# A hybrid attention layer on one core: the end rebuilt, and small work on the vector and scalar engines moved behind other work

## The chip, the cores and the metric

The kernel runs on one core of a Trainium2 chip. Its engines run side by side, each through a fixed list of instructions in order: TensorE (PE, matrix products), VectorE (DVE, elementwise work), ScalarE (ACT, copies, functions, squares with sums), GpSimd (POOL) and SyncE (SP, which here only issues transfers; POOL and ACT issue some too). Semaphores tie the lists together. The metric is the device time of one execution in microseconds (us), as the median of three runs.

## The reference

One decoder layer over 512 tokens of width 2048, in float32. Half of the heads are latent attention (MLA), half are forgetting attention (FoX); both are gated, their outputs go through one projection, and a normalised result is added to x:

```python
h = _rms_norm(x, g_pre)
q_lat, kv_lat, k_rope_raw, gate_mla, fq, fk, fv, f_logit, gate_fox = jnp.split(h @ w_in, split_points, axis=-1)
o_mla = _mla_branch(q_lat, kv_lat, k_rope_raw, ...) * jax.nn.silu(gate_mla)
o_fox = _fox_branch(fq, fk, fv, f_logit, b_forget) * jax.nn.silu(gate_fox)
o = jnp.concatenate([o_mla, o_fox], axis=-1) @ w_out
return x + _rms_norm(o, g_post)
```

In the MLA half, queries, keys and values come from normalised latents (`w_uq`, `w_ukv`), and part of each query and key is rotated by position. In the FoX half, running sums of log-sigmoids of `f_logit` are added to the scores.

## The kernel before

**Arithmetic.** A float32 product is made of three fast products of high and low halves (`mm3`, L153 to L156): high by high, high by low, low by high. Each weight chunk is loaded into `raw`, its high half `whi` is cast by ACT (L295), and its low half `wlo` is the difference that DVE takes (L298). PE meets a chunk first with `whi`, a little later with `wlo`.

**Products.** Four projections go through a scheme with seven block products in place of eight, named p1, p2, p4, q6, g7, g5 and g3: FoX values and gates (`v`, `g`), latents and MLA gate (`l`, `m`), MLA values (`u`) and the output (`o`). Their operands are sums of blocks of x, of latents or of weights, so there are many 128x512 additions and subtractions on DVE between the products.

**Order.** The program is written once, in straight order; a scheduler then makes one static list for each engine from its own estimates of durations. Two things steer it: `in_order` (L136) keeps an instruction where the program has it, and `todo` (L608) is a queue of small steps of which `pump` takes one or two after each group of matmuls, so that a step's place in the program is set by its place in the queue. `wait(n)` hands out pauses.

**The places that matter here**, in the order of time:

- Opening (about 50 to 80 us). The `fq` products run; `todo` gets sums of x (`x_sums`, tiles `rmg`, `smg`) and the log-sigmoid steps `fs` (tile `rft`) from L1329. At the end of the chain PE transposes `rft` into bank `rf` (L878), and DVE copies it out and scans it. Behind `fq` come the products `va` of values from chunks `rawv` and `ga` of gates.
- Latents (about 570 to 580 us). When product g5 of `l` ends, four additions `lc <- ls, lc` (L1400, called from L1461) are issued at once, ahead of the low half of the next chunk; PE then works on MLA-gate products `mg` and on queries `mq` of the first MLA pair.
- First MLA pair (590 to 620 us). `mla_q` (L1727) makes queries, casts and rotates them; then p1 of `u` fills the banks `uA`, which ACT copies to `up`; keys `mk` follow; then q6 (banks `uC`, from operand `suq`), p2 (`uA` again), p4 (`uB`) and g7 (`uC`), with scores `sm` of the heads between.
- Fourth MLA pair (about 702 us). Attention outputs are divided into halves (`boa`) by steps put at the front of `todo` (L1783).
- End (from about 840 us). The last product is p2 of `o` for the second half of the columns, banks `oa10` (token tile 0) and `oa11` (token tile 1). `held=3` keeps its last three weight chunks ready so that tile 0 is ended before tile 1 on them. `finish` (L1857) takes the sum of squares of a row (`sso`), the inverse root y (tile `fin`), multiplies by the gain `gp`, adds x (`xr`) and stores to `out`. The two later token tiles (2 and 3) are finished earlier; tile 0 and then tile 1 come last. For tile 1 the four quarters of the columns are: quarter 0 on PE (x and the scaled values are added in bank `mix`, ACT copies it out), quarters 1, 3 and 2 on DVE (`SCALAR_TENSOR_TENSOR`, below STT: values times y plus x).

Of the kernel before, what the change touches and what calls it, by code (L numbers as in the profile page):

```python
# [19 lines left out]
P = 128  # L20
D = 2048
# [44 lines left out]
def tile_hybrid_layer(  # L66
# [50 lines left out]
    def split(src, name, scale=None, first=0):  # L117

        both = parts_of[name] = slot(name, F32R)
        hi, lo = both[:, 0, :], both[:, 1, :]  # L120
        split_into(hi[:, first:], lo[:, first:], src[:, first:], scale)
        return hi, lo

    def whole_block(wholes, i, src, scale=None):

        to = wholes[:, i // 4, i % 4 * P : (i % 4 + 1) * P]
        if scale is None:
            act.copy(to, src[:, :P])
        else:
            act.mul(to, src[:, :P], scale)  # L130
# [22 lines left out]
    def mm3(o, ah, al, bh, bl, first, last, **kw):  # L153
        pe.matmul(o, ah, bh, start=first, stop=False, **kw)  # L154
# [132 lines left out]
    def divide(i):  # L287
# [4 lines left out]
        hi = wp.tile([P, 1024], F32R, tag="whi", name=f"whi{i}")  # L292
        lo = wp.tile([P, 1024], F32R, tag="wlo", name=f"wlo{i}")
# [157 lines left out]
    for n in ("q0", "p1", "k0", "q6", "p2", "p4", "g7", "q1", "g5", "k1", "g3", "q2", "k2", "q3", "k3"):  # L451
# [184 lines left out]
    def proj_T(rng, outs, kh, kl, rate=1, ahead_load=4):  # L636
# [3 lines left out]
        for i in rng:  # L640
            hi, lo = chunk(i, ahead_load)
            for j in range(chunks[i][3]):
                for o, rows, pick in outs:
                    mm3(o[:rows, :], pick(hi, j), pick(lo, j), kh[k], kl[k], k == 0, k == n_k - 1)
# [190 lines left out]
    def forget_sums(r):  # L835
# [39 lines left out]
        def rows():  # L875
            pt = att_bank("rf")
            for t in range(NT):
                pe.transpose(pt[:n, t * P : (t + 1) * P], r[:, t * n : (t + 1) * n], ident)  # L878
# [156 lines left out]
    def away_steps(of, j, pair, plain=(), keep=None):  # L1035
# [14 lines left out]
        def make(i, n, x, y, names=None):  # L1050
# [3 lines left out]
            dve.tensor_tensor(out=blocks[n], in0=blocks[x], in1=blocks[y], op=ALU.subtract)  # L1054
# [274 lines left out]
    todo.extend([*x_sums(0), *fs[3:], *x_sums(1)])  # L1329
# [94 lines left out]
    def products(gs, names, between, out=lambda g, c, half: None):  # L1424
# [3 lines left out]
        for name in names:  # L1428
            for g in gs:
# [332 lines left out]
    for p in range(4):  # L1762
# [4 lines left out]
        q, qw, wholes = mla_q(p)  # L1767
        if p == 0:
            A = [proj_bank("uA0"), bank("pv", "uA1", 1)]
            up_product("p1", latent_x(0, 0), A, True)  # L1770
            p1 = slot("up1")
            for t in range(2):
                act.copy(p1[:, t, :], A[t])
            p1 = halves(p1)
        elif p == 1:
# [6 lines left out]
        else:  # L1782
            todo.extendleft(divisions("a12", "o"))  # L1783
# [11 lines left out]
        ]  # L1795
        enqueue_scores(heads)
# [250 lines left out]
```

## Time and profile before

| | us |
|---|---|
| Median of three runs (lowest to highest) | 887.06 (886.84 to 887.31) |
| The profiled execution | 887.44 |
| Its span in the profile | 885.6 |
| DVE busy | 643.5 |
| ACT busy | 507.0 |
| POOL busy | 124.3 |
| Granted TensorE clock, mean | 0.999 |

The profile is of one execution. The span runs from the first to the last recorded event; the execution's own time is 1.8 us longer. Records of consecutive matmuls overlap (a matmul of 512 columns is recorded with 0.39 us, but the next one starts 0.227 us after it), so a wait of PE is read from the distance between two starts. In a view of the timeline a row has the start, the duration, the engine, the line, the operation, the tiles (result `<-` operands) and the shapes; `xN` stands for N instructions in one row, and in brackets stands idle time of the engine with what ended it.

### The profile page before, as it was taken

The numbers are of one execution on the slowest core, as the hardware profiler recorded it, in microseconds if no ns is written. First come the engines' busy times: TensorE is split into PE (matmuls) and PEld (weight loads), VectorE is DVE, ScalarE is ACT, GpSimd is POOL, SyncE is SP. The second block draws the span as 40 slices with busy tenths as digits, with TensorE's granted clock in tenths as the row PEclk, the third lists the DMA queues.
The fourth block names the chain that finished last, engine by engine and source line by source line (L and its number), as shares of the span: only waits on it lengthen the run. The fifth ranks groups of instructions, "written<-read, shape, count | busy, mean of one in ns | idle before, by whom it ended". The sixth has DMA issues, their size and how long they took to land.

```text
span 885.6 us, 13146 instructions
## 1 busy us (share of the span) xinstructions
PE 874.2 (99%) x4724; PEld 753.5 (85%) x4724; DVE 643.5 (73%) x1120; ACT 507.0 (57%) x933; POOL 124.3 (14%) x131
## 2 busy tenths in 40 slices
PE   9999999999999999999999999999999999999997
PEld 9988888888888888889999999887888788888885
DVE  4789567778475645547667778899778777998786
ACT  7855444444276553545564455649585986655483
POOL 0024014441010101000024433100000000000030
PEclk9999999999999999999999999999999999999999
DMA  9599879999587898984789999887969537699787
GB/s 291 162 303 276 284 200 195 224 231 238 103 199 216 226 219 208 244 216 131 267 293 239 230 215 258 179 230 164 215 160 246 138 130 253 198 333 331 258 220 236
DMA packets 129158, 198.37 MB, mean 224 GB/s; under 512 B 16370, under 2 KB 62092, under 8 KB 128068
## 3 DMA queue, kind: packets, MB, share of 16 engines
q1 hardware_dynamic: 101956, 136.09, 48.8%
q0 software_dynamic: 26256, 61.02, 35.3%
q8 instruction: 37, 0.61, 0.3%
q10 hardware_dynamic: 880, 0.42, 0.2%
q14 instruction: 29, 0.24, 0.1%
HBM read 182.60 MB, written 44.25 MB: 256 GB/s over the span
## 4 chain that ended last, share of the span: by engine, by line
PE 86%; DVE 6%; ACT 4%; DMA 3%; issue 1%; SPq 0%; DVEq 0%; ACTq 0%
PE gg L1122 3%; PE fk L154 3%; PE fk L156 3%; PE fk L155 3%; PE fq L154 3%; PE fq L156 3%; PE fq L155 3%; PE in L679 2%; PE sm L725 2%; PE lg L1122 2%; DMA rawl<-in_w_in_dram 2%; PE mg L156 2%; PE gg L1123 2%; PE mg L155 2%; PE mg L154 2%; PE ga L1122 2%
## 5 line engine op out<-in xcount | busy, mean ns | idle before, releaser
L298 DVE TENSOR_TENSOR wlo<-raw,whi 128x1024 fp32r<-128x1024 f32 (+3 forms) x159 | 186.7, 1175 | 91.8 <-ACT whi L295 86.6
L295 ACT CAST whi<-raw 128x1024 fp32r<-128x1024 f32 (+3 forms) x158 | 160.0, 1017 | 158.4 <-PE fk L155 43.3
L154 PE MATMUL fk<-h,whi 128*128 128x512 f32 x128 | 51.3, 401 | 0.0
L154 PE MATMUL fq<-h,whi 128*128 128x512 f32 x128 | 50.4, 394 | 0.0
L156 PE MATMUL fk<-h,wlo 128*128 128x512 f32 x128 | 50.1, 392 | 0.0
L156 PE MATMUL fq<-h,wlo 128*128 128x512 f32 x128 | 50.1, 391 | 0.0
L155 PE MATMUL fq<-h,whi 128*128 128x512 f32 x128 | 50.1, 391 | 0.0
L155 PE MATMUL fk<-h,whi 128*128 128x512 f32 x128 | 49.9, 390 | 0.0
L295 ACT CAST whi<-rawv 128x1024 fp32r<-128x1024 f32 x24 | 25.2, 1052 | 37.2 <-PE gg L1122 18.7
L295 ACT CAST whi<-rawl 128x1024 fp32r<-128x1024 f32 x25 | 26.2, 1050 | 35.2 <-PE mg L155 10.4
L298 DVE TENSOR_TENSOR wlo<-rawl,whi 128x1024 fp32r<-128x1024 f32 x25 | 30.5, 1222 | 19.8 <-ACT whi L295 19.8
L295 ACT CAST whi<-rawg 128x1024 fp32r<-128x1024 f32 x24 | 25.3, 1052 | 30.5 <-PE vg L156 15.3
L298 DVE TENSOR_TENSOR wlo<-rawv,whi 128x1024 fp32r<-128x1024 f32 x24 | 29.2, 1219 | 16.5 <-ACT whi L295 16.2
L298 DVE TENSOR_TENSOR wlo<-rawg,whi 128x1024 fp32r<-128x1024 f32 x24 | 29.2, 1222 | 13.1 <-ACT whi L295 13.1
L745 ACT ACTIVATE pf<-pf,stf 128x128 f32<-128x128 f32 (+3 forms) x32 | 17.9, 559 | 22.5 <-DVE stf L736 22.5
L1854 POOL DMA_DIRECT2D c<-in_x_dram x8 | 7.0, 1012 | 168.1 <-ACT c L1853 168.1
L679 PE MATMUL in<-whi,h 128*128 128x328 f32 x128 | 29.8, 326 | 0.0
L247 POOL DMA_DIRECT2D rawl<-in_w_in_dram x20 | 23.9, 1193 | 41.4 <-DVE wlo L298 31.3
L154 PE MATMUL mq<-ln,whi 128*128 128x512 f32 x72 | 29.0, 403 | 0.5 <-ACT whi L295 0.5
L156 PEld LDWEIGHTS fk<-h,wlo 128*128 128x128 f32 x128 | 24.0, 188 | 5.3
L156 PEld LDWEIGHTS fq<-h,wlo 128*128 128x128 f32 x128 | 24.0, 188 | 5.1
L155 PE MATMUL mq<-ln,whi 128*128 128x512 f32 x72 | 28.2, 392 | 0.0
(605 smaller groups left out, 2792.7 us busy)
## 6 DMA issues: line engine op xcount, KB each, us to landing
raw<-in_w_in_dram SPq DMA_DIRECT2D x62, 512.0 KB
raw<-in_w_out_dram SPq DMA_DIRECT2D x32, 512.0 KB
rawl<-in_w_in_dram POOLq DMA_DIRECT2D x20, 512.0 KB, 10.9
rawv<-in_w_in_dram POOLq DMA_DIRECT2D x16, 512.0 KB, 9.0
rawg<-in_w_in_dram POOLq DMA_DIRECT2D x16, 512.0 KB, 10.7
raw<-in_w_in_dram POOLq DMA_DIRECT2D x12, 512.0 KB, 9.8
bmg<-awaymg SPq DMA_DIRECT2D x20, 256.0 KB
rawl<-in_w_in_dram SPq DMA_DIRECT2D x10, 512.0 KB
```

The source lines that it names most:

```text
L154: pe.matmul(o, ah, bh, start=first, stop=False, **kw)
L155: pe.matmul(o, ah, bl, start=False, stop=False, **kw)
L156: pe.matmul(o, al, bh, start=False, stop=last, **kw)
L247: pool.dma_start(to, second, accum_op=ALU.add)
L295: act.copy(hi[:, :m], raw[:, :m])
L298: dve.tensor_tensor(out=lo[:, :m], in0=raw[:, :m], in1=hi[:, :m].bitcast(F32), op=ALU.subtract)
L679: pe.matmul(banks[t][:, :n], a[k][:, tss[t]], b[:, j, :], start=k == 0 and m == 0, stop=k == NK - 1 and m == 2,)
L725: m = pe.matmul(s[:, :nn], a[:, qs], c[:, :nn], start=(i == 0), stop=(i == len(pairs) - 1))
L745: act.activation(p, p, AF.Exp, bias=st[:, 0:1], scale=unit, accum_out=st[:, 1:2])
L1122: pe.matmul(o[t][f], hi[:, j, c], both, start=first and kk == 0, stop=False, skip_group_check=True)
L1123: pe.matmul(o[t][f][:, :HALF], lo[:, j, c], both[:, 0, :], start=False, stop=last and kk == 7, skip_group_check=True,)
L1854: pool.dma_start(to, x[piece(t, c)], accum_op=ALU.add)
```

## The change

Six places of the program are edited.

1. Opening: the steps of `fs` go ahead of all sums of x in `todo`, behind ten empty steps; the transposes into `rf` and the subtractions of the first two sums are kept in program order.
2. Latents: the four additions behind g5 of `l` become steps of `todo`; those of the other projections stay.
3. First MLA pair: p2 and p4 of `u` come ahead of q6 (also in the list by which chunks are loaded); p1's copies are kept in order and put between the casts and the rotation of the queries; the first matmul of each query chain is kept in order; two pauses stand ahead of the scores.
4. Fourth MLA pair: the divisions of `boa` are spread, one in every second place of `todo` from the sixth on.
5. Last chunk: its halves get tiles of their own in the freed pool `op`, so that they needn't wait for a `whi` and a `wlo` to come free; `held` is 4; one bank (`oh1`) for a gained value goes, and the value stays in its own tile.
6. `finish`: the root is taken by ACT straight from the sum (scale and bias in the instruction), while DVE computes v; y is then 2w/(w² + v) in place of 1/w with one Newton step. Tile 0: quarters 3 and 2 on DVE, 0 and 1 as an ACT multiplication and a POOL addition each. Tile 1: three pieces of 256 columns on PE and ACT, five on DVE; the gain of quarter 2 stands ahead of its two pieces.

```diff
-    todo.extend([*x_sums(0), *fs[3:], *x_sums(1)])
+    todo.extend([*[lambda: None] * 10, *fs[3:], *x_sums(0), *x_sums(1)])
...
-                pe.transpose(pt[:n, t * P : (t + 1) * P], r[:, t * n : (t + 1) * n], ident)
+                in_order(pe.transpose(pt[:n, t * P : (t + 1) * P], r[:, t * n : (t + 1) * n], ident))
...
-                    put(g, 1, 0, a, ALU.add)
-                    put(g, 1, 1, a, ALU.add)
+                    adds = [lambda g=g, c=c, a=a: put(g, 1, c, a, ALU.add) for c in range(2)]
+                    if g == "l":
+                        todo.extend(adds)
+                    else:
+                        for add in adds:
+                            add()
...
-    for n in ("q0", "p1", "k0", "q6", "p2", "p4", "g7", "q1", "g5", "k1", "g3", "q2", "k2", "q3", "k3"):
+    for n in ("q0", "p1", "k0", "p2", "p4", "q6", "g7", "q1", "g5", "k1", "g3", "q2", "k2", "q3", "k3"):
...
-            up_product("p1", latent_x(0, 0), A, True)
             p1 = slot("up1")
-            for t in range(2):
-                act.copy(p1[:, t, :], A[t])
+            def first_up():
+                up_product("p1", latent_x(0, 0), A, True)
+                for t in range(2):
+                    in_order(act.copy(p1[:, t, :], A[t]))
+            q, qw, wholes = mla_q(p, first_up)
...
-            todo.extendleft(divisions("a12", "o"))
+            for i, s in enumerate(divisions("a12", "o")):
+                todo.insert(6 + 2 * i, s)
...
+        if i < len(chunks) - 1:
+            hi = wp.tile([P, 1024], F32R, tag="whi", name=f"whi{i}")
+            lo = wp.tile([P, 1024], F32R, tag="wlo", name=f"wlo{i}")
+        else:
+            hi, lo = (more[0].tile([P, 1024], F32R, tag="raw", name=f"w{n}{i}", bufs=3) for n in ("hi", "lo"))
...
-    product("p2", 1, operand("a12", "o"), A2, False, True, held=3, side=[end2])
+    product("p2", 1, operand("a12", "o"), A2, False, True, held=4, side=[end2])
```

The core of the new `finish`:

```python
        act.activation(w, sso[:, t, 3:4], AF.Sqrt, bias=u, scale=1.0 / D)
        dve.tensor_scalar(out=v, in0=sso[:, t, 3:4], scalar1=1.0 / D, scalar2=u, op0=ALU.mult, op1=ALU.add)
        in_order(dve.tensor_scalar(out=q, in0=w, scalar1=w, scalar2=v, op0=ALU.mult, op1=ALU.add))
        in_order(dve.reciprocal(q, q))
        in_order(dve.tensor_scalar(out=y, in0=q, scalar1=w, scalar2=2.0, op0=ALU.mult, op1=ALU.mult))
...
        if t < LAST:
            done(3, whole)
            gained()
            done(2, whole)
            for c in (0, 1):
                act.mul(homes[c], og[t][c], y)
                pool.tensor_tensor(out=homes[c], in0=homes[c], in1=xr[t][c], op=ALU.add)
                nc.sync.dma_start(out[piece(t, c)], homes[c])
            return
        mixes = [(proj_bank("mix0"), 1, left), (proj_bank("mix1"), 0, left), (att_bank("mix2"), 0, right)]
...
        for mix, c, at in mixes:
            act.copy(homes[c][:, at], mix[:, :HALF])
            act.dma_start(out[piece(t, c)][:, at], homes[c][:, at])
        done(1, right)
        done(3, left)
        done(3, right)
        gained()
        done(2, left)
        done(2, right)
```

Three places of the static lists, before and after. DVE in the opening, before: `rft` is the log-sigmoid chain, `rmg` and `smg` are sums of x, `wlo` low halves of weights, `rf` the copy of the transposed result.

```order
L864 RECIPROCAL rft_647<-rft_647 128x32
L298 TENSOR_TENSOR wlo13_784<-rawv0_678,whi13_783 128x1024
L848 TENSOR_TENSOR rft_647<-rft_647 128x32
L1054 TENSOR_TENSOR rmg51_819<-xr01_618,xr11_619 128x512
L848 TENSOR_TENSOR rft_647<-rft_647 128x32
L845 TENSOR_SCALAR rft_647<-rft_647 128x32
L1054 TENSOR_TENSOR rmg51_819<-xr01_618,rmg51_819 128x512
L848 TENSOR_TENSOR rft_647<-rft_647 128x32
L144 TENSOR_TENSOR smg51_821<-rmg51_819,smg51_821 128x512
L848 TENSOR_TENSOR rft_647<-rft_647 128x32
L1054 TENSOR_TENSOR rmg31_833<-xr11_619,rmg51_819 128x512
L851 SCALAR_TENSOR_TENSOR rft_647<-rft_647 128x4x8
```

After, from the same point of the chain (the reciprocal):

```order
L868 RECIPROCAL rft_647<-rft_647 128x32
L852 TENSOR_TENSOR rft_647<-rft_647 128x32 x2
L849 TENSOR_SCALAR rft_647<-rft_647 128x32
L852 TENSOR_TENSOR rft_647<-rft_647 128x32 x2
L855 SCALAR_TENSOR_TENSOR rft_647<-rft_647 128x4x8
L302 TENSOR_TENSOR wlo13_774<-rawv0_678,whi13_773 128x1024
L849 TENSOR_SCALAR rft_647<-rft_647 128x4x8
L883 COPY rf_167<-rf_802 72x512
L302 TENSOR_TENSOR wlo14_813<-rawv1_680,whi14_812 128x1024
L889 SCALAR_TENSOR_TENSOR fz_808<-rf_167,fz_808 8x512
L1058 TENSOR_TENSOR rmg50_823<-xr00_528,xr10_529 128x512
L143 TENSOR_TENSOR smg50_825<-rmg50_823,smg50_825 128x512
```

The sums of x stood between the steps of the chain; now the chain runs through, and the first of them stand behind the copy of `rf`, a chunk's low half and the scan `fz`.

ACT in the first MLA pair, before. `up` is p1 of `u` copied out of the banks `uA`, `suq` and `sug` are operands of q6 and g7, `rq` the rotated queries, `mw` and `mk` parts of the keys, `mc` a gate function behind the table load.

```order
L143 CAST rq0_5963<-raq0_5955 64x512 x2
L143 CAST suq60_5985<-ruq60_5941 128x512
L143 CAST sug30_5999<-rug30_5988 128x512
L1773 COPY up1_6004<-uA0_5968 128x512
L1773 COPY up1_6004<-uA1_5969 128x512
L143 CAST sug70_6024<-rug70_6002 128x512
L128 COPY mw0_5952<-mk00_6007 128x128
L128 COPY mw0_5952<-mk01_6008 128x128
L143 CAST mk00_6055<-mk00_6007 128x512
L143 CAST mk01_6058<-mk01_6008 128x512
L295 CAST whi160_6068<-raw160_5873 128x1024
L295 CAST whi161_6151<-raw161_5915 128x1024
```

After, from the copies of `up` on, to the copy `u11` that empties the first `uA` bank after p2:

```order
L299 CAST whi160_6066<-raw160_5876 128x1024
L127 COPY mw0_5955<-mk01_6008 128x128
L299 CAST whi161_6125<-raw161_5918 128x1024
L142 CAST rq0_6002<-raq0_5994 64x512 x2
L142 CAST sug70_6024<-rug70_5990 128x512
L811 ACT_TABLE_LOAD
L811 ACTIVATE mc0_4139<-ghm0_6027 128x512
L811 ACTIVATE mc0_4139<-ghm1_6037 128x512
L142 CAST mk00_6055<-mk00_6007 128x512
L142 CAST mk01_6058<-mk01_6008 128x512
L748 ACTIVATE stm00_6085<-stm00_6085,qcol_3813 128x1
L1820 COPY u11_6118<-uA0_5828 128x512
```

The cast of `suq` stood behind two casts of `rq`, right ahead of the copies `up`; now it stands ahead of the copies `up`, six places ahead of the first row shown, and the copy `u11` stands behind `whi161`, two casts of `rq`, one of `sug`, the table load, two gate functions and the casts of `mk`.

DVE in the last stretch, before: `fin0` and `fin1` are the small columns for the root of tiles 0 and 1, `xr` is x, `oa10` and `oa11` are the last product.

```order
L1913 SCALAR_TENSOR_TENSOR og20_8661<-oa10_7285,fin0_8709,xr02_8652 128x512
L1913 SCALAR_TENSOR_TENSOR c121_8287<-c121_8287,fin0_8709,xr02_8652 128x512
L1913 SCALAR_TENSOR_TENSOR c120_8022<-c120_8022,fin0_8709,xr00_8649 128x512
L1864 TENSOR_SCALAR fin1_8748<-sso_7280,fin1_8748 128x1
L1866 TENSOR_SCALAR fin1_8748<-fin1_8748 128x1
L1872 TENSOR_TENSOR oa11_7286<-oa11_7286,gp1_7282 128x128
L1875 RECIPROCAL fin1_8748<-fin1_8748 128x1
L1877 TENSOR_SCALAR fin1_8748<-fin1_8748 128x1
L1878 TENSOR_SCALAR fin1_8748<-fin1_8748 128x1
L1901 SCALAR_TENSOR_TENSOR c120_8022<-oh1_8553,fin1_8748,xr10_8655 128x256 x2
L1872 TENSOR_TENSOR oa11_7286<-oa11_7286,gp1_7282 128x384
L1913 SCALAR_TENSOR_TENSOR c121_8287<-oh3_8682,fin1_8748,xr12_8658 128x512
```

After, from the first STT of tile 0:

```order
L1896 SCALAR_TENSOR_TENSOR c121_8287<-c121_8287,fin0_8700,xr02_8649 128x512
L1892 TENSOR_TENSOR oa10_7285<-oa10_7285,gp1_7282 128x512
L1896 SCALAR_TENSOR_TENSOR og20_8658<-oa10_7285,fin0_8700,xr02_8649 128x512
L1884 TENSOR_SCALAR fin1_8745<-sso_7280,fin1_8745 128x1
L1885 TENSOR_SCALAR fin1_8745<-fin1_8745 128x1
L1886 RECIPROCAL fin1_8745<-fin1_8745 128x1
L1887 TENSOR_SCALAR fin1_8745<-fin1_8745 128x1
L1896 SCALAR_TENSOR_TENSOR c120_8022<-c120_8022,fin1_8745,xr10_8652 128x256
L1896 SCALAR_TENSOR_TENSOR c121_8287<-oh3_8667,fin1_8745,xr12_8655 128x256 x2
L1892 TENSOR_TENSOR oa11_7286<-oa11_7286,gp1_7282 128x512
L1896 SCALAR_TENSOR_TENSOR og20_8658<-oa11_7286,fin1_8745,xr12_8655 128x256 x2
```

The third STT of tile 0 is gone from DVE, as are one small column step and the gain of 128 columns between the root's steps; tile 1 has one STT of 256 columns on `c120` where there were two.

More of the change, by code (lines that the diff above doesn't have):

```diff
@@ L151, in split_into, with mm3 @@
             in_order(a, b)
-    def mm3(o, ah, al, bh, bl, first, last, **kw):
-        pe.matmul(o, ah, bh, start=first, stop=False, **kw)
+    def mm3(o, ah, al, bh, bl, first, last, pin=False, **kw):
+        i = pe.matmul(o, ah, bh, start=first, stop=False, **kw)
+        if pin:
+            in_order(i)
         pe.matmul(o, ah, bl, start=False, stop=False, **kw)
@@ L1868, in finish @@
+        homes = [og_tile(t, c) for c in range(4)]
         og[t][last] = o
-        sides = (slice(0, P), slice(P, S)) if t == LAST else (slice(0, S),)
-        def gain_side(at):
-            return dve.tensor_tensor(out=o[:, at], in0=o[:, at], in1=gp[last][:, at], op=ALU.mult)
-        in_order(gain_side(sides[0]))
-        dve.reciprocal(y, w)
-        dve.tensor_scalar(out=w, in0=y, scalar1=y, scalar2=h, op0=ALU.mult, op1=ALU.mult)
-        dve.tensor_scalar(out=y, in0=w, scalar1=1.5, scalar2=y, op0=ALU.add, op1=ALU.mult)
@@ L1879, in finish @@
-        if t == LAST:
-            mix = att_bank("mix")
-            scaler = op.tile([P, P], F32, tag="sc", name="scaler", bufs=1)
-            pe.matmul(mix, ident, xr[t][0], start=True, stop=False)
-            busy = att_bank("busy")
-            for n in (S, HALF):
-                pe.matmul(busy[:, :n], ident, xr[t][1][:, :n], start=True, stop=True)
-            act.mul(scaler, ident, y)
-            pe.matmul(mix, scaler, og[t][0], start=False, stop=True)
-        order = enumerate((0, 1, 3, 2))
@@ new lines, in finish @@
+        mixes = [(proj_bank("mix0"), 1, left), (proj_bank("mix1"), 0, left), (att_bank("mix2"), 0, right)]
+        scaler = op.tile([P, P], F32, tag="sc", name="scaler", bufs=1)
+        for mix, c, at in mixes:
+            pe.matmul(mix[:, :HALF], ident, xr[t][c][:, at], start=True, stop=False)
+        busy = att_bank("busy")
+        pe.matmul(busy[:, :HALF], ident, xr[t][1][:, left], start=True, stop=True)
+        act.mul(scaler, ident, y)
+        for mix, c, at in mixes:
+            pe.matmul(mix[:, :HALF], scaler, og[t][c][:, at], start=False, stop=True)
@@ L1994, in end @@
         sub(v, G, halves(v), ALU.add)
-        done_with(0, 2 * g + 1, halves(v), {1: home})
+        done_with(0, 2 * g + 1, halves(v), {1: home} if home is not None else {})
     C = [proj_bank(f"oc{t}") for t in range(2)]
@@ L2003, in tile_hybrid_layer @@
     product("g3", 0, operand("g3", "o"), G, False, True)
-    end(0, v, G, bank("pv", "oh1", 1))
+    end(0, v, G, None)
     product("g3", 1, operand("g3", "o"), G2, False, True)
```

92 lines of the change are left out of this document (42 added, 50 removed).

## The prediction

> **What bounds the kernel.** I read the page first, then the waits of PE, then the timeline around each wait.
>
> ```profile
> span 885.6 us, 13146 instructions
> PE 874.2 (99%) x4724; PEld 753.5 (85%) x4724; DVE 643.5 (73%) x1120; ACT 507.0 (57%) x933; POOL 124.3 (14%) x131
> ...
> PE uC L154 <- ACT suq L143: 1.6, 1, 1.6
> ...
> PE mix L1888 <- ACT scaler L1887: 1.0, 1, 1.0
> PE mk L154 <- ACT mw L128: 0.7, 1, 0.7
> PE mq L154 <- ACT whi L295: 0.5, 1, 0.5
> PE rf L878 <- DVE rcol L1547: 0.3, 1, 0.3
> PE pvm L154 <- DVE mc L776: 0.2, 1, 0.2
> ```
>
> PE works through 99% of the span, and the change takes no product away. So there are only two stocks to win from: these waits, some 4 us together, and the tail behind the last product. Each of the edits aims at one row. The sum is made against the profiled execution, 887.44 us (the span of 885.6 and 1.84 around it); the median is 887.06, so 0.38 comes off at the end.
>
> **Opening.**
>
> ```profile
> 54.52 0.34 DVE L864 RECIPROCAL rft<-rft 128x32 f32<-128x32 f32 x1
> 58.86 0.69 DVE L1054 TENSOR_TENSOR rmg<-xr 128x512 f32<-128x512 f32 x1
> 59.46 0.17 DVE L845 TENSOR_SCALAR rft<-rft 128x32 f32<-128x32 f32 x1
> ...
> 59.08 0.39 PE L156 MATMUL fq<-h,wlo 128*128 128x512 f32 x1
> 59.78 0.38 PE L878 MATMUL rf<-ident,rft 128*72 128x128 f32 x2 [0.31 <-DVE rcol L1547]
> ...
> 69.30 1.22 DVE L298 TENSOR_TENSOR wlo<-rawv,whi 128x1024 fp32r<-128x1024 f32 x1
> 73.41 0.39 PE L155 MATMUL va<-wlo,h 128*128 128x512 f32 x1
> ```
>
> From 59.08 to 59.78 are 0.70 us where a 512-column matmul takes 0.23 to the next start, so PE loses 0.47. Between the reciprocal and the last step of `rft` (54.52 to 59.46) DVE makes five sums of x like that of 58.86, 0.6 to 0.7 each. Without them the chain ends over 3 us earlier, so the 0.47 goes. The eight sums come back behind the scan, where DVE makes the halves of the `va` chunks. By my reckoning the half of 69.30 then ends near 72.9 in place of 70.5, and PE asks for it near 73.4 (73.41, less 0.47, plus two matmuls by which the new order of PE asks later). That cover of half a microsecond is thin, and the next half, for `ga`, has no more. Value 0.45; range 0 (each tenth that DVE is later there comes back as a wait) to 0.55.
>
> **Latents.**
>
> ```profile
> 570.15 2.48 DVE L1400 TENSOR_TENSOR lc<-ls,lc 128x512 f32<-128x512 f32 x4
> 572.55 1.21 DVE L298 TENSOR_TENSOR wlo<-raw,whi 128x1024 fp32r<-128x1024 f32 x1
> ...
> 571.44 0.28 PE L155 MATMUL mg<-bmg,whi 128*128 128x256 f32 x1
> 572.22 0.50 PE L154 MATMUL mq<-ln,whi 128*128 128x512 f32 x1 [0.50 <-ACT whi L295]
> ```
>
> PE breaks off `mg` at 571.44, since the low half it wants next is made only at 572.55, behind four additions that take 2.48; it goes over to `mq`, which waits too. From 571.08 to 579.90 PE issues 48 matmuls of 256 columns (0.12 each) and 9 of 512 (0.23): 7.83 of 8.82 us, so 0.99 is lost. With the additions behind the half, that half is ready near 571.3. But ACT's high half of the next chunk and the `mq` behind it stay where they are, and about half of the loss with them. Value 0.5; range 0 to 1.0.
>
> **First MLA pair.** This is the largest wait, and the least certain term.
>
> ```profile
> 599.03 0.39 PE L156 MATMUL mk<-ln,wlo 128*128 128x512 f32 x1
> 601.01 0.50 PE L154 MATMUL uC<-whi,suq 128*128 128x512 f32 x1 [1.59 <-ACT suq L143]
> ...
> 599.05 1.26 ACT L143 CAST rq<-raq 64x512 fp32r<-64x512 f32 x2 [3.94 <-DVE raq L1735]
> 603.17 1.10 ACT L143 CAST mk<-mk 128x512 fp32r<-128x512 f32 x2
> 604.12 2.04 ACT L295 CAST whi<-raw 128x1024 fp32r<-128x1024 f32 x2
> 606.18 1.28 ACT L807 ACT_TABLE_LOAD   x1
> 607.48 1.16 ACT L807 ACTIVATE mc<-ghm 128x512 f32<-128x512 f32 x2
> ...
> 599.26:609.54 10.28, 8.69 (x43) 6.96 (x43) 10.15 (x16) 10.12 (x17) 0.00 (x0) 1.00 0.46 84
> ```
>
> (The last row is a window: length, then busy time of PE, weight loads, DVE, ACT and POOL.) PE loses 1.75 at 601.01 because `suq` stands behind `rq`, and `rq` behind the rotation; with small losses up to 609 it is 2.3. Now p2 comes first and needs only ready latents; `suq` has four more microseconds. So this wait goes. What is late next is the end of the same group. By the order, the second bank of `uC` is `uA`'s old one: it waits for the copy `u11`. ACT takes `whi161` only when PE has ended p2, whose `whi158` it overwrites: p2's twelve matmuls start from 599.26 on, the last at 601.75, and with its 0.39 that is 602.15. Then follow, start to start, `whi161` 1.0, two `rq` 1.25, `sug` 0.5, the table load 1.3, two `mc` 1.1, two `mk` 0.95, a small step 0.25 and the copy itself 0.5: 6.9, so the bank is free near 609.1. PE gets there after p2, p4 and half of q6, 30 matmuls from 599.26, or 606.1, with 0.5 of scores between (and one wait of 0.5 for DVE's maximum): 607.1. The new wait is 2.0, with the 0.5 it is 2.5, against 2.3. The window says why: DVE and ACT are both busy for 98% of this stretch, so a new order of PE can hardly shorten it. Value −0.2; range −1.5 to +2.0 (the upper end if the copy is not waited for).
>
> [...] The rows show the load at 606.18 and the next function at 607.48, 1.30 apart, and no drain ahead of it (the casts of 604.12 end at 606.16). [...]
>
> **Fourth pair.**
>
> ```profile
> 702.36 0.63 ACT L143 CAST boa<-boa 128x512 fp32r<-128x512 f32 x1
> ```
>
> PE's wait for `mw` (0.7) and for `mc` (0.2) stand in the first fence: `boa` casts of 0.5 each are in ACT's way. Spread out, they leave the first place but come later, ahead of scores' work; the chunk that follows is then as late as before. Value 0.2; range −0.3 to 0.6.
>
> **The end.**
>
> ```profile
> 875.07 1.68 POOL L1911 TENSOR_TENSOR og<-og,xr 128x512 f32<-128x512 f32 x1 [12.06 <-issue]
> 875.54 1.76 DVE L1913 SCALAR_TENSOR_TENSOR c<-c,fin,xr 128x512 f32<-128x512 f32 x1
> 876.40 0.19 ACT L1839 ACTIVATION_READ_ACCUMULATOR osq<-oa 128x1 f32 x1
> 877.22 0.20 DVE L1864 TENSOR_SCALAR fin<-sso,fin 128x1 f32<-128x1 f32 x1
> 877.46 0.20 ACT L1865 ACTIVATE fin<-fin 128x1 f32<-128x1 f32 x1 [0.86 <-DVE fin L1864]
> 877.72 0.15 DVE L1875 RECIPROCAL fin<-fin 128x1 f32<-128x1 f32 x1
> 877.91 0.27 DVE L1877 TENSOR_SCALAR fin<-fin 128x1 f32<-128x1 f32 x1
> 878.22 0.21 DVE L1878 TENSOR_SCALAR fin<-fin 128x1 f32<-128x1 f32 x1
> 878.47 0.88 DVE L1901 SCALAR_TENSOR_TENSOR c<-oh,fin,xr 128x256 f32<-128x256 f32 x2
> 878.93 1.12 PE L1888 MATMUL mix<-og,scaler 128*128 128x512 f32 x2 [0.96 <-ACT scaler L1887]
> ...
> 881.28 0.35 ACTq L1905 DMA_DIRECT2D out_dram<-og  x1
> ...
> 881.45:883.40 1.95, 0.00 (x0) 0.00 (x0) 0.00 (x0) 0.00 (x0) 0.00 (x0) 1.00 1.02 362
> ```
>
> The sum of squares is there at 876.59, yet the root begins at 877.22: DVE is held by an STT of tile 0 that took 1.76 beside POOL's addition. Now tile 0's sum closes 24 matmuls (5.4 us) ahead of the last, not 18; its third STT goes to ACT and POOL, and DVE is free near 874.3. So root and v both start at 876.65. The steps then take 0.26 (root), 0.31, 0.19 and 0.25, in the spacings of the rows: y's first user starts at 877.65, not 878.47. From there five STTs of 256 columns (0.4 each) and a gain of 512 (0.6) end near 880.3; on the other side scaler 0.46, three PE pieces of half the 1.12 each, copies and issues put the last issue of ACT near 880.6, against 881.28. The stores behind it flow at 362 GB/s until 883.40 (the last row), because the view of DMA issues has 768 KB in the last four, from 880.5 on; now 512 KB are in the last four, spread over 0.7 us and issued earlier, and they are through near 882.3. Value 1.1; range 0.4 (only the earlier y, with a late bank or low half) to 1.4. A fourth held chunk asks for its low half 1.4 us earlier; I find it ready with 0.1 to spare.
>
> [...] If any DVE work beside POOL were stretched as in the row of 875.54, it would be 0.4.
>
> **Sum.** 0.45 + 0.5 − 0.2 + 0.2 + 1.1 = 2.05 less; 887.44 − 2.05 − 0.38 = **885.0**.
>
> **Rivals.** (1) The copy `u11` is not waited for, or comes early: then 2.2 more, 882.8. For it: the wait that goes is the profile's largest. Against: the order of ACT. (2) Opening and latents give nothing, the waits move on to the `va`, `ga` and `mq` halves: 0.95 less gain, 886.0. For it: DVE's thin cover of half a microsecond. (3) The tail keeps its length, because tile 0's POOL additions, two in place of one, reach into tile 1's STTs (1.02 more, as in the row of 875.54): 886.0. Against: they should end by 876.5. [...] (5) Slower: DVE, at 98% between 599 and 609, becomes the bound, because the rotation (six operations) now stands ahead of the low halves `wlo159` and `wlo160` for PE's next products. Each microsecond that DVE lags is one of PE. Up to 2 us the wait at `u11` hides it; from 4 us of lag the gains elsewhere are used up. At 6 us it is 889.0.
>
> **Chances.** Forecast 50%, (1) 15%, (2) 11%, (3) 8%, (4) 4%, (5) 12%. About 0.2% (1.8 us) is what a measurement of this kernel can tell from no change; the border is 885.3, inside the forecast's own range of 884.2 to 885.9, of which I put 60% below. Faster: 30 + 15 = 45%. Same: 20 + 11 + 8 + 4 = 43%. Slower: 12%. The range leaves out (5) and half of (1): 882.9 to 887.1.
>
> **What would show it.** Right: no gap ahead of `rf`; `mg` unbroken at 571; a wait of about 2 us of `uC` on ACT's `u11`; the first STT of tile 1 1.25 us behind the start of the sum's read-out (876.40 here), not 2.07; last issue about 0.7 earlier. Wrong: PE waits at `wlo` of `va` or `ga`, at `uB` or `uC` on a low half, or a stretched STT of tile 1.

## The result: slower by 0.7%, and the profile after

| | before | after |
|---|---|---|
| Median, us (lowest to highest of nine runs each) | 887.06 (886.65 to 891.31) | 893.61 (890.74 to 895.60) |
| Ratio after to before, with its 95% interval | | 1.0066 (1.0055 to 1.0077) |
| The profiled execution, us | 887.44 | 893.61 |
| Its span, us | 885.6 | 891.8 |

The kernel became slower, by 6.5 us in the medians and 6.2 us in the two profiled spans. The page and the waits of PE after the change (line waited for, us in total, times, longest):

```profile
span 891.8 us, 13167 instructions
...
PE 876.2 (98%) x4730; PEld 755.7 (85%) x4730; DVE 642.2 (72%) x1114; ACT 507.5 (57%) x936; POOL 125.3 (14%) x132
```

```profile
PE ga L1128 <- ACT whi L299: 4.1, 1, 4.1
PE uC L153 <- ACT u L1820: 1.7, 1, 1.7
...
PE mg L157 <- DVE wlo L302: 1.1, 1, 1.1
PE mix L1925 <- ACT scaler L1923: 0.6, 1, 0.6
```

The wait at `rf` is gone, `uC` waits for `u11` (the `u` of L1820) in place of `suq`, and the wait of `mix` is shorter: so far as predicted. At the top stands a wait that the prediction hasn't: `ga` for the high half of a weight chunk. Cutting both traces at the same PE instructions tells what it cost. Each row is the difference of two starts (the last one ends with the span, which runs to 885.63 and 891.84):

| stretch | before | after | difference |
|---|---|---|---|
| start to first `va` | 65.03 | 63.97 | −1.06 |
| first `va` to first `vg` | 44.40 | 52.48 | +8.08 |
| first `vg` to last `lg` | 455.79 | 455.92 | +0.13 |
| last `lg` to first `uG` (latents, first pair) | 71.63 | 71.87 | +0.24 |
| first `uG` to last `oa` (with the fourth pair) | 238.58 | 238.64 | +0.06 |
| last `oa` to the end | 10.21 | 8.96 | −1.25 |
| sum | | | +6.20 |

So the end gave what was hoped for, the middle gave nothing, and the opening lost 7. (Of the 1.06 in the first row only 0.50 comes behind the input products; the other 0.56 is there when the last `in` starts, at 41.07 in place of 41.63, which no edit touches.)

What happened between `va` and `vg` is a chain over four engines. First PE and ACT in the timeline after the change:

```profile
97.62 0.39 PE L157 MATMUL va<-whi,h 128*128 128x512 f32 x1
102.07 0.79 PE L1128 MATMUL ga<-h,whi 128*128 128x512 f32 x1 [4.07 <-ACT whi L299]
103.33 0.58 PE L1129 MATMUL ga<-h,wlo 128*128 128x256 f32 x1 [0.47 <-DVE wlo L302]
...
116.45 0.40 PE L153 MATMUL vg<-whi,smg 128*128 128x512 f32 x1
...
100.97 1.04 ACT L299 CAST whi<-raw 128x1024 fp32r<-128x1024 f32 x1 [8.79 <-DMA raw<-in_w_in_dram]
```

PE stops for 4.22 us beyond its step of 0.23, because ACT's cast comes at 100.97; ACT itself was idle 8.79 us for the load of that chunk. Why the load is late stands in the waits of SP's queue between 60 and 110 us, after the change and before it:

```profile
SPq L260 <- DMA awaymg<-rmg: 31.6, 3, 22.0
```

```profile
SPq L259 <- DVE wlo L298: 13.3, 1, 13.3
...
SPq L259 <- DMA awaymg<-rmg: 9.4, 1, 9.4
```

SP waits 22.0 us for a single store of a sum of x (`awaymg`, from `rmg` to DRAM), 9.6 of them ahead of the store's own issue; before, its longest wait of that kind was 9.4. In the timelines of POOL and SP after the change, and then of SP before it (four loads in one row, with the time from the start of the first issue to the end of the last):

```profile
81.96 1.07 POOL L1048 DMA_DIRECT2D awaymg<-rmg  x1
...
94.41 4.54 SPq L260 DMA_DIRECT2D raw<-in_w_in_dram  x4
```

```profile
84.02 13.67 SPq L259 DMA_DIRECT2D raw<-in_w_in_dram  x4
```

Of the eight `raw` loads of this stage the last four were issued between 84.02 and 97.7 before, and between 94.41 and 98.95 after: the first of them, which is the fifth of the eight, comes ten microseconds later. The static list of SP says what it waits for (rows of the two lists, not of a profile; DMASW is a transfer on POOL's queue, DMAHW one on SP's own):

```
before  44 L259 DMA raw_1091<-in_w_in_dram 128x2x512 [waits DMAHW7_49,DMAHW3_49,DVE_49]
after   44 L260 DMA raw_1091<-in_w_in_dram 128x2x512 [waits DMAHW7_49,DMASW5_49,DVE_49]
```

Before, this load took the buffer of an earlier weight chunk, once DVE had made its low half. After, it takes the buffer of a sum of x (`rmg`), and so waits for that sum's store to land. The sums had been moved behind the scan, their stores with them; the store is issued on POOL's queue between two weight loads, at 81.96, and SP stands until 94.41. The trace has the landing of this store at 94.36, so the load goes 0.05 us behind it. It is 0.05 again in three more traces with the same order (`e2_alone`, `e4_fill` and `e5_fill16`, described below), while the DVE step nearest to the issue ends anywhere from 0.3 ahead of it to 0.1 behind it; so it is the store that releases the load, not DVE. The loads behind it on SP's queue, which `ga` needs too, follow at 94.88, 95.43 and 98.58.

Last, the windows after the change (length, then busy time of PE, weight loads, DVE, ACT and POOL, then the granted clock, the DMA share and GB/s):

```profile
80.00:96.00 16.00, 16.00 (x82) 13.62 (x81) 13.93 (x20) 5.83 (x9) 4.12 (x5) 1.00 1.11 254
...
100.00:101.00 1.00, 0.00 (x0) 0.00 (x0) 0.00 (x0) 0.03 (x1) 0.00 (x0) 0.93 1.03 272
101.00:107.00 6.00, 4.46 (x13) 3.48 (x14) 3.68 (x3) 3.98 (x5) 1.44 (x2) 0.50 0.91 329
107.00:108.00 1.00, 1.00 (x6) 0.86 (x6) 0.00 (x0) 0.00 (x0) 0.00 (x0) 0.65 0.91 311
```

The DMA engines are full from 80 to 96 (a share of 1.11), and the store takes 12.4 us. But neither is new: before the change the share in this stretch was 1.08, and a store of a sum issued at 82.87 took 13.8 us to land (96.63); the load that waited for it was the seventh of the eight, issued at 96.77. What is new is that the fifth load hangs on such a store. And the pause has a second price: the granted clock falls to 0.50 at about 100.9 and comes back at about 107.7. The 18.83 us from the last `va` to the first `vg` are 7.31 more than before (11.52): 4.22 for the first wait, 1.03 for the second (1.26 between the starts less 0.23), and 2.06 left for the slow clock. The other 0.77 of the 8.08 in the table lie between the first and the last `va`, where PE waits for two low halves that DVE makes later than before; the first of these waits:

```profile
70.06 0.50 PE L156 MATMUL va<-wlo,h 128*128 128x512 f32 x1 [0.26 <-DVE wlo L302]
```

### The profile page after: what moved, and what is told of

It is laid out like the page before. It is cut to its first block, busy times and chain, and to the rows that moved or that the text cites. A ratio compares the mean times of both kernels' runs of the same rounds, so it can differ in the third digit from the quotient of the medians.

```text
span 891.8 us, 13167 instructions
## 1 busy us (share of the span) xinstructions
PE 876.2 (98%) x4730; PEld 755.7 (85%) x4730; DVE 642.2 (72%) x1114; ACT 507.5 (57%) x936; POOL 125.3 (14%) x132
## 4 chain that ended last, share of the span: by engine, by line
PE 81%; DVE 7%; ACT 6%; DMA 4%; issue 2%; SPq 0%; DVEq 0%; ACTq 0%
PE in L683 3%; PE gg L1128 3%; PE fk L153 3%; PE fk L156 3%; PE fk L157 3%; PE lg L1128 2%; PE fq L153 2%; PE fq L157 2%; PE fq L156 2%; DMA raw<-in_w_in_dram 2%; PE sm L729 2%; DVE wlo L302 2%; PE oc L153 2%; PE od L156 2%; PE vg L153 2%; PE vg L157 2%
## 5 line engine op out<-in xcount | busy, mean ns | idle before, releaser
L153 PE MATMUL mq<-ln,whi 128*128 128x512 f32 x72 | 28.9, 401 | 0.0
L1128 PE MATMUL ga<-h,whi 128*128 128x512 f32 x64 | 24.7, 424 | 4.1 <-ACT whi L299 4.1
```

The lines of the kernel that those rows point to most:

```text
L153: i = pe.matmul(o, ah, bh, start=first, stop=False, **kw)
L1128: pe.matmul(o[t][f], hi[:, j, c], both, start=first and kk == 0, stop=False, skip_group_check=True)
```

## The experiments

Theory T is the chain above: late sums, a late store, a load that waits for it at the head of SP's queue, PE idle, a slow clock. The rivals are named in each expectation. Times are medians; each ratio is against the kernel before on the same chip (886.97, 887.45, 887.56 and 887.37 in the four groups e1 to e4, e5 to e8, e9 to e11, e12).

**The opening's edit taken out, and alone.** `e1_undo` is the changed kernel with the old opening:

```diff
-    todo.extend([*[lambda: None] * 10, *fs[3:], *x_sums(0), *x_sums(1)])
+    todo.extend([*x_sums(0), *fs[3:], *x_sums(1)])
-                in_order(pe.transpose(pt[:n, t * P : (t + 1) * P], r[:, t * n : (t + 1) * n], ident))
+                pe.transpose(pt[:n, t * P : (t + 1) * P], r[:, t * n : (t + 1) * n], ident)
-            if of == "m" and j < 2:
-                in_order(it)
```

> The changed kernel with the opening's order (and its pins) put back, all other edits kept. Theory T, that the loss is made in the opening, because the load of a weight chunk now stands at the head of SP's queue behind the landing of a late store of a sum of x: the products vg start 7.0 us earlier than in the changed kernel, 109.4 in place of 116.4, no wait of ga above 1 us, clock 0.999, time 886.3 (885.8 to 886.9). Rival R, that the loss is made by the first MLA pair or spreads over the kernel: time above 889.

Measured: 886.24, ratio 0.9988 (0.9975 to 1.0000). The waits of `ga` are gone and that of `rf` is back; the clock stays at 1.00. `e2_alone` is the kernel before with the same lines changed the other way, and nothing else:

> The kernel before with the edit of the opening alone. T: the same wait of ga on ACT's high half (3 to 5 us) and the same fall of the granted clock, vg from 116.4 on, time 894.1 (892 to 896). R: time 886.6 to 887.2.

Measured: 894.67, ratio 1.0087 (1.0072 to 1.0102). Its waits of PE and of SP's queue show the same pair:

```profile
PE ga L1124 <- ACT whi L295: 3.2, 1, 3.2
```

```profile
SPq L259 <- DMA awaymg<-rmg: 30.9, 3, 21.4
```

So the whole loss comes from the opening's edit: alone it costs 0.87%, and without it the other five edits leave the kernel about 0.1% faster (an interval that just reaches 1.0000).

**The stores on another queue.** `e3_act` is the changed kernel with the sums' stores issued by ACT:

```diff
-            pool.dma_start(to.rearrange("p (h c) -> p h c", c=HALF), src)
+            (act if of == "m" else pool).dma_start(to.rearrange("p (h c) -> p h c", c=HALF), src)
```

> The changed kernel, order of the opening kept, but the stores of the sums of x for the MLA gate go out on ACT's queue instead of POOL's. T: no load of raw waits for a store that stands behind POOL's loads; SP issues the chunks of ga near 85 instead of 94 to 98, ga waits less than 1 us, vg starts near 109, time 886 (885.3 to 887.5). Rival D, that the sums themselves are too late on DVE for the weight halves, whoever stores them: ga still waits, time above 889.

Measured: 889.11, ratio 1.0026 (1.0013 to 1.0040), so more than half of the loss is gone. The wait of 4 us has become several small ones, SP's longest wait for a store fell from 22.0 to 7.3, and the first `vg` starts at 112.91, not 116.45:

```profile
SPq L260 <- DMA awaymg<-rmg: 23.4, 5, 7.3
```

```profile
101.96 0.50 PE L1128 MATMUL ga<-h,whi 128*128 128x512 f32 x1 [0.32 <-ACT whi L299]
103.22 0.39 PE L1129 MATMUL ga<-h,wlo 128*128 128x256 f32 x1 [0.76 <-DVE wlo L302]
```

This run alone can't tell the queue from the buffer: the fifth load also got another buffer. It is issued at 86.12, behind a low half that ends at 86.10 and not behind a store. The rest of the loss is halves that are late on DVE and loads that still wait for other stores. The time of 889.11 misses T's 886 and lies where rival D was put, so DVE's late sums have a part in it.

**The sums only a little later.** `e8_noempty` is the changed kernel without the ten empty steps; the sums still stand behind the scan, and the stores on POOL's queue:

```diff
-    todo.extend([*[lambda: None] * 10, *fs[3:], *x_sums(0), *x_sums(1)])
+    todo.extend([*fs[3:], *x_sums(0), *x_sums(1)])
```

> The changed kernel without the ten empty steps: fs first, then all sums of x at once. By the lists the fifth load behind rawg on SP's queue now takes a buffer that no store to DRAM has to leave. Theory T (the chain: late store, a load that waits for it at the head of SP's queue, late halves): no wait of 4 us at ga, the granted clock stays at 1.00, vg's first near 109 to 111, 885.5 to 888. Rival R (DVE's low halves are late because the sums stand behind the scan, whatever the stores do): waits of va and ga for low halves remain as in the run with the stores on another queue, vg near 113, 889.

Measured: 887.26, ratio 1.0000 (0.9991 to 1.0009). In its list the fifth load waits for an earlier weight chunk's buffer again, and the four loads are issued from 85.59 on. No wait of 4 us is left, only one low half:

```profile
85.59 14.56 SPq L260 DMA_DIRECT2D raw<-in_w_in_dram  x4
```

```profile
105.52 0.39 PE L1129 MATMUL ga<-h,wlo 128*128 128x256 f32 x1 [0.76 <-DVE wlo L302]
```

That is what T expects, and not the 889 of its rival. The sums come up to ten steps earlier here, so DVE's part isn't quite held fixed; but they still stand behind the scan, and the loss goes with the load's wait for the store. The edit still wins nothing: the first `va` comes 23.20 us behind the last `in` (23.40 before), and from the last `va` to the first `vg` it takes 12.50 in place of 11.52, because of that low half.

**What the clock costs.** Unused matmuls of 128 columns ahead of the second pass of `ga` keep PE busy in the pause (they add work and leave none out). First 36 of them, then 16:

```diff
+        if g == "g":
+            fill_bank = att_bank("fill")
+            for i in range(16):
+                in_order(pe.matmul(fill_bank[:, :P], warm, warm, start=True, stop=True))
```

> The changed kernel with 36 matmuls of 128 columns on constants put ahead of ga's second pass, where PE waits; their result is used by nothing. T with the wait as cause of the lower clock: whi of that chunk is as late as before (102.0), but the clock stays at 1.00 behind it, ga's 128 columns of work run at full speed, vg starts 2.5 us earlier than in the changed kernel, time 891.0 (889.5 to 892). Rival C, that the clock falls for another reason than PE's idle time: clock 0.5 again from 101 on, time 893 to 895.

Measured: 893.63, ratio 1.0075 (1.0060 to 1.0090); the clock stayed at 1.00, but the time missed the forecast. Each of the 36 is recorded twice (72 records, 8.20 us busy) and took twice the time reckoned: they ran from 98.83 to 106.78, 0.22 us each, beyond the end of the wait. The cause of the clock's fall was shown, its price was not. Hence the second run:

> The changed kernel with 16 unused matmuls of 128 columns ahead of ga's second pass (it adds work, it takes none away). In the run with 36, they took 0.114 us for each half, 8.2 us in all, from 98.83 to 106.78, past the end of the wait for the late chunk, so nothing could be saved there. Sixteen take 3.6 us and end near 102.4, where the late high half is ready in the changed kernel (102.0). If the fall of the granted clock to 0.50 after the idle 4 us costs time of its own, the first vg comes near 114.5 in place of 116.45 (one wait of 0.5 to 1.0 for the low half stays, then 32 pairs of ga at 0.35 each) and the kernel takes 891.7. If the clock costs nothing, because the halves that ga wants are as late anyway, vg stays at 116.4 and the time at 893.6.

```profile
98.13 3.73 PE L1489 MATMUL fill<-warm 128*128 128x128 f32 x32
103.18 0.39 PE L1129 MATMUL ga<-h,wlo 128*128 128x256 f32 x1 [0.76 <-DVE wlo L302]
```

Measured: 890.74, ratio 1.0039 (1.0025 to 1.0052). The first `vg` starts at 114.15 (114.5 expected): 2.3 earlier than in the changed kernel, and 2.06 was the rest in the account above. Counted from that late low half (its user starts at 103.18 here, at 103.33 in the changed kernel) to the first `vg`, it is 10.97 in place of 13.12, so 2.15 less. So of the 7.3 between `va` and `vg` some 2 are the slow clock.

**The end alone, and with the old root.** `e6_end` is the kernel before with the edits 5 and 6 of the change only:

> The kernel before with the edits of the end alone (finish, the last chunk's own tiles, held 4, one bank less). By the account of the changed kernel's trace the distance from the last matmul of oa to the end of the span shrinks from 10.21 to 8.96, so 1.2 less than before: 885.8. By the prediction's term 1.1: 885.9. If part of this came only from what stood ahead of it in the changed kernel, between 886.2 and 887.0.

Measured: 886.24, ratio 0.9989 (0.9980 to 0.9998), 1.2 less in the medians. (886.24 as such lies in the last branch, but the kernel before took 0.4 longer on this chip; by the difference it is the first.) The span ends 8.9 behind the last `oa` (876.18 to 885.1). `e11_root` is the same with the root taken as before:

```diff
-        act.activation(w, sso[:, t, 3:4], AF.Sqrt, bias=u, scale=1.0 / D)
+        act.sqrt(w, v)
-        in_order(dve.tensor_scalar(out=q, in0=w, scalar1=w, scalar2=v, op0=ALU.mult, op1=ALU.add))
-        in_order(dve.reciprocal(q, q))
-        in_order(dve.tensor_scalar(out=y, in0=q, scalar1=w, scalar2=2.0, op0=ALU.mult, op1=ALU.mult))
+        in_order(dve.tensor_scalar(out=q, in0=v, scalar1=-0.5, scalar2=None, op0=ALU.mult))
+        in_order(dve.reciprocal(y, w))
+        in_order(dve.tensor_scalar(out=w, in0=y, scalar1=y, scalar2=q, op0=ALU.mult, op1=ALU.mult))
+        in_order(dve.tensor_scalar(out=y, in0=w, scalar1=1.5, scalar2=y, op0=ALU.add, op1=ALU.mult))
```

> The edits of the end alone, but with the root as before: v on DVE first, then ACT's root of v, 1/w and one Newton step (the new sharing of the last tile, tile 0's ACT and POOL pieces, held 4 and the last chunk's tiles stay). If the 1.2 of the end comes mostly from tile 0's work being out of DVE's way, the start of v is as early as in the changed kernel and only the longer chain comes back, some 0.25: the tail behind oa's last matmul is 9.2 and the time 886.5 against 886.2 of the end alone. If the new root brings most of it, the tail is 9.7 or more and the time 887.

Measured: 888.09, ratio 1.0003 (0.9994 to 1.0011). The tail is 9.2 (877.99 to 887.2), as the first branch says, but the time is 1.6 above it. The trace puts that ahead of the tail, in waits that the end alone doesn't have:

```profile
PE oa L155 <- DVE wlo L301: 0.5, 1, 0.5
PE od L155 <- DVE wlo L301: 0.4, 1, 0.4
```

The last `oa` starts 33.9 us behind the last `oc`, against 32.6 in both other kernels. So with the old root the tail is 0.25 longer, and in this execution 1.3 are lost ahead of it, behind the last `oc`, and another 1.0 between the first `uG` and the last `oc`. It is the slowest of the eleven (888.94); how much of that belongs to the root in the median, two runs on two chips don't tell. That DVE's pinned steps, which wait for ACT's root, hold up those low halves is my reading; no run took them apart.

**Latents and first pair, each by itself.** `e7_nolat` is the run e1 with the latents' additions put back; `e9_lat` is the kernel before with their edit alone; `e10_pair` the kernel before with edit 3 alone.

```diff
-                    adds = [lambda g=g, c=c, a=a: put(g, 1, c, a, ALU.add) for c in range(2)]
...
+                    put(g, 1, 0, a, ALU.add)
+                    put(g, 1, 1, a, ALU.add)
```

> The changed kernel with the opening's order and the four additions behind g5 of the latents put back; first pair, fourth pair and end stay. If the latents' edit costs 0.3, as the marks of the trace say, 885.9 against 886.2 of the run without the opening's edit alone. If it gains 0.5, as predicted, 886.7.

> The kernel before with the latents' edit alone (the four additions behind g5 of l as steps of todo). The prediction's term: 0.5 less, 886.9 against 887.4 on the chip used last, and no wait of mq for a high half. Against it, what the changed kernel's trace shows: mg waits 0.6 to 1.1 for a low half instead, and nothing is won, 887.4 to 887.7. From the first matmul of the last lg group to the first of uG the kernel before takes 71.6.

> The kernel before with the first pair's edit alone (p2 and p4 of u ahead of q6, the copies of p1 ahead of the rotation, the two pauses). The prediction's term: 0.2 more, with a wait of 2.0 of uC's second bank for ACT's copy u11 in place of 1.6 for suq: 887.6 against 887.4. Rival: the copy is not waited for, as in the run without the opening's and the latents' edits, where no wait of uC stands and the stretch from the end of lg to uG is 70.6 in place of 71.6: 886.4.

Measured: e7 886.23, ratio 0.9984 (0.9976 to 0.9993); e9 887.29, 1.0002 (0.9993 to 1.0010); e10 887.02, 0.9997 (0.9987 to 1.0007). By the medians neither edit is worth anything that can be told from zero. The marks show where PE lost time in one execution of each (lost time is the sum over matmul starts of what exceeds their usual step):

| | lost, last `lg` to first `uA` | last `lg` to first `uA` | first `uA` to first `uG` |
|---|---|---|---|
| before | 1.07 | 25.88 | 45.75 |
| e9, latents alone | 1.70 | 26.38 | 45.92 |
| e10, pair alone | 4.38 | 29.13 | 44.02 |
| e7, pair and end | 1.83 | 26.58 | 44.03 |
| e1, pair, latents and end | 1.00 | 25.71 | 45.60 |
| after | 1.51 | 26.21 | 45.66 |

Runs with the same edits at this place show how far one execution can be trusted: from the last `lg` to the first `uA` they take 24.95 (e8) to 26.29 (e3) with the edits of the latents and the pair, and 25.55 (e2) to 26.17 (e6) with neither. So only the 29.13 and the two 44.0 stand out. With the pair's edit and the old latents PE wins 1.7 behind `uA` and loses ahead of it, 3.25 in e10 and 0.7 in e7: the queries' first matmuls are now pinned, and PE stands at a low half where it used to go over to `mq`. In the timelines of e10 and of e7:

```profile
574.24 0.39 PE L157 MATMUL mg<-bmg,wlo 128*128 128x256 f32 x1 [2.52 <-DVE wlo L299]
```

```profile
573.90 0.39 PE L157 MATMUL mg<-bmg,wlo 128*128 128x256 f32 x1 [1.48 <-DVE wlo L302]
```

The execution of e10 in the profile took 888.98, 2.0 above the median of its run, so the longer stall needn't be the usual one; in e7 1.0 of the gain is left from `lg` to `uG`. In e10 and e7, with the old latents, `uC` then has no wait for `u11`; in e1 and after, with the new ones, PE loses less ahead and has that wait of 1.7. That DVE is the reason, and that PE waits at the next place for what it gains at one, is likely from the window of this stretch before the change (DVE is the fourth time, 26.07 of 27 us), but no run took it apart.

```profile
565.00:592.00 27.00, 26.50 (x166) 23.48 (x165) 26.07 (x41) 16.58 (x27) 0.00 (x0) 1.00 0.75 209
```

**A version that is faster.** `e12_nopin` is e7 (the old opening and latents; pair, fourth pair and end new) without the pin:

```diff
-        proj_T(mla[p]["q"], [(qb[i], P, cols(i * P)) for i in range(3)], qnh, qnl, 2, 6, p == 0)
+        proj_T(mla[p]["q"], [(qb[i], P, cols(i * P)) for i in range(3)], qnh, qnl, 2, 6)
```

> The run without the edits of the opening and the latents, now also without the pin on the first matmul of each query chain. Pins theory: in the first pair's edit alone PE stops 2.7 us (1.6 in the run with the end) in mg at a low half, because the pinned mq may no longer be taken ahead of it; without the pin mq comes first again, the stall from the last lg to the first uA falls from 1.8 to about 1.1, as before the change, and that stretch from 26.6 to 25.9. If the later stretch (uA to uG, 44.0 with p2 first and no wait for u11) keeps its length, lg to uG is 70 in place of 71.6 and the time 885.2 to 885.8 against 887.5 before. DVE theory: DVE is busy for 26.1 of 27 us there, so what PE wins ahead of uA it waits for later, at u11 or a low half: uA to uG is 45.5 again, lg to uG 71.3 and the time 886.2, as with the end alone.

Measured: 885.31, ratio 0.9974 (0.9964 to 0.9984), the best of all, 2.1 less in the medians. The time is that of the pins theory. The profiled execution is not: `mq` does come first again, with a short wait,

```profile
573.16 0.50 PE L153 MATMUL mq<-ln,whi 128*128 128x512 f32 x1 [0.37 <-ACT whi L299]
```

and 25.47 us from `lg` to `uA`, but `uA` to `uG` is 45.15, together 70.62, as in e7 (70.61). This execution is the slowest of the nine (886.19), and it loses 1.28 between the last `va` and the first `vg` (12.80 in place of 11.52), where none of its edits lie. What makes the 2.1 stands in the traces of both e7 and e12: 1.0 from `lg` to `uG` and 1.1 to 1.25 behind the last `oa`. The intervals of e7 and e12 overlap, so whether the pin itself costs anything stays open; that e12 beats the kernel before doesn't.

## Why the prediction was wrong

Forecast 885.0, range 882.9 to 887.1; measured 893.61. The step that failed is the opening: "**Value 0.45; range 0 (each tenth that DVE is later there comes back as a wait) to 0.55.**" It was −7, and the runs e1 and e2 put 7.4 and 7.7 of the miss of 8.6 there.

- **What was right in it.** PE's gap ahead of `rf` went, and was worth 0.50.
- **What was left out.** The step counted DVE's operations alone: eight sums that come back where DVE makes halves. Each sum that moved also has a store behind it, on POOL's queue, and a buffer that stays taken until the store has landed (here 94.36, and the load at 94.41). I followed neither the store nor the next user of the buffer, a weight load at the head of SP's queue. The row that priced it was in the profile before: `SPq L259 <- DMA awaymg<-rmg: 9.4`, a wait of SP for just such a store. It said that loads of this stage already hang on these stores. On DVE's side the step was off too, by less: the half reckoned for 72.9 ended at 73.56, PE wanted it at 73.4 as forecast, and an earlier half was late by 0.4. These waits make the 0.77 in `va`; they are the kind that rival 2 and the signs of being wrong had.
- **The bound.** "Range 0 to 0.55" took a delay of tenths as the worst. The chain through a transfer went far beyond it: 12.4 us of landing, 4.2 of idle PE, and 2 more of slow clock. None of the rivals had a load behind a store; the slower one was put into DVE at 599 to 609, where nothing of it was seen.
- **Latents: 0.5 forecast, nothing measured** (e9: 1.0002, 0.9993 to 1.0010). The first low half does come earlier, at 577.20 after the change, 2.5 earlier than before when both are counted from the last `lg`. The next one isn't: it stands behind two of the moved additions and a step that waits for ACT (`[0.73 <-ACT ln L142]`), and PE waits there instead:

```profile
578.99 1.29 DVE L1406 TENSOR_TENSOR lc<-ls,lc 128x512 f32<-128x512 f32 x2
581.01 0.69 DVE L143 TENSOR_TENSOR ln<-lat,ln 128x512 fp32r<-128x512 f32 x1 [0.73 <-ACT ln L142]
581.62 1.22 DVE L302 TENSOR_TENSOR wlo<-raw,whi 128x1024 fp32r<-128x1024 f32 x1
...
582.89 0.39 PE L157 MATMUL mg<-bmg,wlo 128*128 128x256 f32 x1 [1.05 <-DVE wlo L302]
```

The forecast of "about half" kept back the `mq` behind ACT's half, but didn't follow the moved additions to the next low half, which they now stand ahead of. In the changed kernel the pin of edit 3 also keeps `mq` from filling in, but that isn't what decides: e9 has no pin, PE does go over to `mq` at 574.76, and it still waits for this second half:

```profile
576.43 0.39 PE L156 MATMUL mg<-bmg,wlo 128*128 128x256 f32 x1 [1.27 <-DVE wlo L298]
```

- **First pair: −0.2 forecast, right in mechanism; its size is not shown.** Alone (e10) it gives nothing that can be told from zero (0.9997, 0.9987 to 1.0007), as forecast, but that run has no wait for `u11` and lost its time at `mg`: there the agreement is luck. In the changed kernel the mechanism is the one forecast. The bank was to be free near 609.1. PE reached this stage 7.48 later (first `uA` at 598.57, not 591.09), which makes 616.6, and that is what the timeline has, with ACT's casts, table load and copy in the order reckoned:

```profile
612.61 1.28 ACT L811 ACT_TABLE_LOAD   x1
...
613.91 1.15 ACT L811 ACTIVATE mc<-ghm 128x512 f32<-128x512 f32 x2
...
616.10 0.59 ACT L1820 COPY u<-uA 128x512 f32<-128x512 f32 x1
...
616.74 0.49 PE L153 MATMUL uC<-whi,suq 128*128 128x512 f32 x1 [1.66 <-ACT u L1820]
```

The load and the next function stand 1.30 apart, as in the rows before the change. Rival 1, no wait at `u11`, does occur (e7, e10), but doesn't bring its 2.2: in e10 PE has lost more than that ahead of it, and in e7 1.0 is left in the trace.
- **Fourth pair: 0.2 forecast.** It was not run alone. The wait of `mk` for `mw` (0.7) did go, and the first `oa` starts 68.94 behind the first `uG` in place of 69.38; but a new wait followed in scores' work (`pvm` for `phm`, 0.3), as forecast, and of the 0.44 only 0.12 is left when `ob` starts (118.52 in place of 118.64). To the last `oa` the trace has 0.06 more after the change, so no gain can be seen.
- **The end: 1.1 forecast, 1.25 in the trace**, and 1.2 alone (e6). The first STT of tile 1 was to come 1.25 behind the start of the sum's read-out; it is 1.31, with root and v both starting at 884.03, and the last issue comes 0.75 earlier behind the last `oa` (0.7 forecast):

```profile
883.80 0.19 ACT L1858 ACTIVATION_READ_ACCUMULATOR osq<-oa 128x1 f32 x1
884.03 0.29 ACT L1883 ACTIVATE fin<-sso,fin 128x1 f32<-128x1 f32 x1
884.03 0.22 DVE L1884 TENSOR_SCALAR fin<-sso,fin 128x1 f32<-128x1 f32 x1 [2.15 <-ACT osq L1858]
...
885.11 0.48 DVE L1896 SCALAR_TENSOR_TENSOR c<-c,fin,xr 128x256 f32<-128x256 f32 x1
```

Rival 3 falls: tile 0's second POOL addition ends at 883.13, two microseconds ahead of tile 1's first STT, which takes 0.48.

## What to carry to other kernels

When a step moves, list what it issues as well as what it computes: the store behind it, the buffer that the store holds, and whoever takes that buffer next. If that is a load with others behind it on its queue, the price of a small delay is everything queued there: here four loads, issued from 94.41 on in place of 84.02. So look in the profile before for waits of the load queue on a store, however small: they show which loads hang on stores. And where an engine is busy for 97% of a stretch, expect that a new order of another engine mostly moves its waits: here 1.7 won at one place came with 0.7 to 3.25 lost at another.

## What was not expected of the hardware

- A pause of PE of 4.1 us (98.0 to 102.1) halved the granted clock, from 1.00 to 0.50, from about 100.9 to 107.7: 6.8 us, 5.6 of them after work had come back. The fall came 2.9 us behind PE's last work. With unused matmuls in the pause the clock stayed at 1.00 (`e4_fill` and `e5_fill16`).
- The clock also fell behind a much shorter wait. In `e5_fill16` the wait of `uC` for `u11` took 1.66, as in the changed kernel, but there the clock fell to 0.50 behind it, and from the first `uA` to the first `uG` it took 47.14, not 45.66. Ahead of the fall PE was busy for 1.65 of 3.41 us (the first time behind the length in the rows below). In the changed kernel it was busy for 1.57 of the 3.30 us up to the end of that wait (613.40 to 616.70), and the clock stayed at 1.00; what decides between the two isn't shown.

```profile
609.96:613.37 3.41, 1.65 (x9) 1.03 (x8) 3.38 (x8) 3.41 (x9) 0.00 (x0) 1.00 0.92 284
613.40:616.70 3.30, 3.30 (x13) 3.02 (x12) 1.79 (x7) 3.03 (x10) 0.86 (x1) 0.50 0.34 137
```

- A store of 512 KB issued by POOL at 81.96 held SP until 94.41: it took 12.4 us to land, with the DMA engines at a share of 1.11. The eight stores of these sums in that trace took 6.0 to 12.4 us, 8.3 in the median.
- Nine runs of the changed kernel spread over 4.9 us (890.74 to 895.60), where eight of the nine of the kernel before lie within 1.2 (886.65 to 887.83). The landing of that store hardly explains it: in four traces with this order it took 11.7 to 12.4. The granted clock goes with the time in part: it was 0.998 in the fastest of the nine and 0.994 in each of the three slowest (894.07 to 895.60), but lowest, 0.993, in a run of 893.18.
